# Hybrid diffusion backbone on one core: modulation moved from the HGRN heads to the merge of D, half of its sums on VectorE, a D chunk between two forget gates

## The chip, the core and the metric

The kernel runs as one program on one core of a Trainium2 chip. The metric is device time in microseconds of one execution; less is better. Engines are named as in the profile: PE (TensorE), DVE (VectorE), ACT (ScalarE), POOL (GpSimd) and SP (SyncE, here the queue that issues most DMAs).

## The reference, cut to what matters

Two trunk layers run on 640 tokens (128 of a prompt, 512 of a sample). The prompt and the sample have their own condition vector, so every modulation coefficient exists twice.

```python
for l in range(DEPTH):                                   # DEPTH = 2, D_MODEL = 1024
    mod = silu(cvec) @ w_ada + b_ada                     # (1024) @ (1024, 3072): shift, scale, gate
    h = x * (1 + scale) + shift
    z = h @ w_in + b_in                                  # 92 chunks of 128 columns
    # A: HGRN, 4 heads: q, i, g and two forget gates ff, fb; a gated scan over the tokens, both ways
    out_a = hgrn(a_q, a_ff, a_fb, a_i, a_g)
    out_b = neighbourhood_attention(b_q, b_k, b_v) * silu(b_g)
    out_c = mla(c_qd, c_kvd, c_kpe) * silu(c_g)
    out_d = d_b * short_conv(d_c * d_x) * silu(d_g)      # 4 chunks of 128 columns
    mixed = sum(sigmoid(merge_n) * (out_n @ w_branch[n]) for n in "ABCD") @ w_out
    x = layer_norm(ALPHA * x + gate * mixed)
```

## The kernel before

Activations lie transposed, 128 features by 640 tokens, in tiles that are split in two column halves of 384 and 256 (`HALVES`). Matrix products run at full float32 quality in three passes: every weight chunk is split by `split` (L160 on ACT, L161 on DVE) into a high part `whi` and a low part `wlo`, and `zmm` (L217) issues for each of 8 row blocks high by high, high by low and low by high, 24 matmuls for a column half. `zchunk` makes one chunk of z that way: it calls `tick`, takes one of two PSUM buffers `g`, issues the 24 matmuls and hands the result to an eviction function, for each half. `mm3` (L208) does the same for the branch and output products.

Side work runs in generators, the streams. Each `tick` advances every stream whose waiting count has run down; a `yield n` asks for n ticks. `hg_mix` (the scan of one HGRN head, 27 ticks), `mla_mix`, `na_all` and `mods` are streams; their instructions stand in the order of the program between two halves of a z chunk. [...]

A layer goes so: four heads, each with its z chunks (`hg_z`) and then its scan as a stream; the D chunks (`branch_d`, four z chunks each) stand after the heads by the table `D_AT`: chunk 0 after head 0, 1 and 2 after head 1, 3 after head 2. Before head h, `need(hgs[h - 2])` ticks until that scan is over. Then the merge of D (8 chunks: a merge gate chunk, then a branch product), the MLA projections, the merge of A, the attention projections, and the merges of C and B, and the output phase.

A forget gate (`ff` in `hg_z`) puts much on DVE for each half: a TENSOR_SCALAR (L447), a RECIPROCAL (L449), a multiply (L450), in layer 1 two more (L453, L454). Head 0 of a layer finds q, i and g made ahead, so that its two gates ff(0) and ff(1) follow each other. A silu eviction is L261 and L262 on DVE behind a Tanh on ACT. In the scan, `ks` (L477) is the first DVE work, PE multiplies it at L489, and each of seven levels has a copy on ACT (L499), a predicated copy (L507) and products (L512 to L518) on DVE.

The modulation `mod_group` makes 512 columns of `silu(c) @ w_ada`: 8 loads of 128x512 (`raw`, L379, from SP's queue), each multiplied by the coefficient of the prompt (j = 0) and of the sample (j = 1) on ACT (L382) and added to two accumulators on POOL (L384), one load a tick; then 8 small matmuls against ones (L391) sum over the partitions. During layer 0 the stream `mods` makes 6 groups (the gates of layer 0, shift and scale of layer 1), during layer 1 two. The stream is added ahead of the first head. The results are needed at `need(mods)`, ahead of the output phase. The tiles `t` (2,560 bytes a partition) come from a pool of `NT_SLOT` slots; a load into a slot waits until the slot's last reader is done.

## Time and profile before

| | us |
|---|---|
| median of 3 runs | 2163.67 (2161.42 to 2163.8) |
| the profiled execution, its own time | 2160.13 |
| span of its instructions | 2158.3 |
| PE busy in the span | 2094.6 (97%) |
| DVE busy | 1387.3 (64%) |
| ACT busy | 904.5 (42%) |
| POOL busy | 273.0 (13%) |
| mean granted TensorE clock | 0.991 |

The span is the time from the first to the last instruction; 1.8 us of the execution lie around it. The share of busy time is an average over stages with different limits, so a stage is read by its own rows.

### The profile page before, as it was taken

The page shows a single profiled execution, that of the slowest core. Times are in us where ns is not written, and L with a number is a line of the kernel's source. Part 1 is how long each engine was busy: PE and PEld are TensorE (multiplying, and loading weights), DVE is VectorE, ACT ScalarE, POOL GpSimd, SP SyncE. Part 2 cuts the span into 40 slices and gives each one's busy share as a digit, 9 for nine tenths or more (in the row PEclk, how much of TensorE's full clock was granted, in tenths as well). Part 3 has the DMA queues.
Part 4 walks back from the last instruction along what each step waited for, and adds up shares of the span by engine and source line. Part 5 has one row for each costly group of instructions (what it writes and reads, how often), then busy time and mean ns, then how long its engine had stood idle before and what let it go on. Part 6 is the DMA issues. An engine that isn't in the chain of part 4 may idle for free.

```text
span 2158.3 us, 35747 instructions
## 1 busy us (share of the span) xinstructions
PE 2094.6 (97%) x14538; PEld 2052.8 (95%) x14538; DVE 1387.3 (64%) x2592; ACT 904.5 (42%) x1587; POOL 273.0 (13%) x212
## 2 busy tenths in 40 slices
PE   7999999999999999999998999999999999999997
PEld 4899999999999999999988899999999999999997
DVE  6897878646655567734588877764475546775456
ACT  4445543323334466523364332332343345653332
POOL 0444451000000023200015200000000002221000
PEclk9999999999999999999999999999999999999998
DMA  7332331122112221222433212112121222221251
GB/s 279 111 110 92 113 114 50 62 73 65 58 57 73 73 62 57 67 72 85 142 120 100 74 62 74 57 57 69 62 75 53 68 59 66 69 68 59 74 166 50
DMA packets 70485, 178.06 MB, mean 82 GB/s; under 512 B 7984, under 2 KB 20912, under 8 KB 70320
## 3 DMA queue, kind: packets, MB, share of 16 engines
q1 hardware_dynamic: 67440, 169.32, 24.3%
q10 hardware_dynamic: 2880, 6.45, 0.9%
q8 instruction: 114, 1.87, 0.4%
q14 instruction: 51, 0.42, 0.1%
HBM read 168.20 MB, written 7.54 MB: 81 GB/s over the span
## 4 chain that ended last, share of the span: by engine, by line
PE 80%; DVE 12%; DMA 3%; ACT 2%; issue 2%; POOL 1%; SPq 0%; ACTq 0%; DVEq 0%; POOLq 0%
PE g L217 47%; PE g L208 15%; PE mx L504 2%; DVE wlo L161 2%; PE mx L744 2%; DMA t<-in_wada 2%; PE mx L959 2%; PE mx L208 1%; PE mx L782 1%; DVE s L449 1%; PE mx L926 1%; PE mx L560 1%; PE mx L217 1%; DVE t L161 1%; PE mx L758 1%
## 5 line engine op out<-in xcount | busy, mean ns | idle before, releaser
L217 PE MATMUL g<-h_hi,whi 128*128 128x256 f32 (+1 forms) x2880 | 907.5, 315 | 21.8 <-DVE e L261 10.4
L217 PE MATMUL g<-h_lo,whi 128*128 128x256 f32 (+1 forms) x2880 | 893.9, 310 | 1.1 <-DVE h_lo L409 0.7
L217 PE MATMUL g<-h_hi,wlo 128*128 128x256 f32 (+1 forms) x2880 | 892.7, 310 | 0.6 <-DVE wlo L161 0.6
L217 PEld LDWEIGHTS g<-h_hi,whi 128*128 128x128 f32 x2880 | 549.5, 191 | 27.9 <-DVE e L261 11.9
L217 PEld LDWEIGHTS g<-h_lo,whi 128*128 128x128 f32 x2880 | 550.1, 191 | 3.3 <-DVE h_lo L409 1.5
L217 PEld LDWEIGHTS g<-h_hi,wlo 128*128 128x128 f32 x2880 | 549.4, 191 | 1.0 <-DVE wlo L161 1.0
L161 DVE TENSOR_TENSOR wlo<-wraw,whi 128x1024 fp32r<-128x1024 f32 (+1 forms) x258 | 294.0, 1140 | 312.9 <-ACT whi L160 311.7
L160 ACT CAST whi<-wraw 128x1024 fp32r<-128x1024 f32 (+1 forms) x258 | 242.5, 940 | 443.6 <-PE g L217 250.9
L208 PE MATMUL g<-t,whi 128*128 128x256 f32 (+1 forms) x1280 | 283.4, 311 | 0.0
L882 POOL TENSOR_SCALAR u<-u,sm 128x320 f32<-128x320 f32 (+2 forms) x80 | 90.1, 1137 | 1230.2 <-DVE sm L880 770.7
L208 PEld LDWEIGHTS g<-t,whi 128*128 128x128 f32 x1280 | 214.5, 189 | 0.5
L384 POOL TENSOR_TENSOR t<-t 128x512 f32<-128x512 f32 x112 | 173.4, 1573 | 272.7 <-ACT t L382 272.5
L208 PE MATMUL g<-t,wlo 128*128 128x384 f32 (+1 forms) x640 | 197.7, 309 | 0.0
L208 PEld LDWEIGHTS g<-t,wlo 128*128 128x128 f32 x640 | 121.1, 189 | 0.0
L382 ACT ACTIVATE t<-t,cf 128x512 f32<-128x512 f32 x128 | 90.5, 719 | 71.4 <-DMA t<-in_wada 70.2
L997 ACT ACTIVATE e<-g,hbin 128x384 f32<-128x384 f32 (+1 forms) x128 | 67.1, 524 | 126.8 <-PE g L217 126.7
L504 PE MATMUL mx<-s,t 128*128 128x128 f32 x560 | 78.5, 289 | 1.4 <-DVE s L516 1.3
L504 PEld LDWEIGHTS mx<-s,t 128*128 128x128 f32 x560 | 74.0, 194 | 2.3 <-ACT e L260 1.6
L260 ACT ACTIVATE e<-g,hbin 128x384 f32<-128x384 f32 x76 | 39.9, 525 | 86.1 <-PE g L217 77.1
L449 DVE RECIPROCAL s<-e 128x384 f32<-128x384 f32 (+1 forms) x32 | 68.7, 2147 | 0.6
L261 DVE TENSOR_SCALAR e<-g,vecs 128x384 f32<-128x384 f32 x76 | 41.2, 542 | 39.3 <-ACT e L260 38.9
L807 ACT ACTIVATE t<-mx,sm,rq 128x640 f32<-128x640 f32 (+1 forms) x40 | 31.9, 798 | 70.2 <-DVE sm L804 60.4
(280 smaller groups left out, 2678.1 us busy)
## 6 DMA issues: line engine op xcount, KB each, us to landing
wraw<-in_win SPq DMA_DIRECT2D x184, 512.0 KB, 3.5
t<-in_wada SPq DMA_DIRECT2D x64, 256.0 KB, 3.9
wraw<-in_wbr SPq DMA_DIRECT2D x64, 256.0 KB, 2.6
wraw<-in_wout SPq DMA_DIRECT2D x20, 512.0 KB, 4.3
s<-in_wada SPq DMA_DIRECT2D x16, 512.0 KB, 6.8
s<-in_nabias SPq DMA_DIRECT2D x8, 640.0 KB, 4.7
m<-in_xT SPq DMA_DIRECT2D x8, 320.0 KB, 8.0
t<-in_xT ACTq DMA_DIRECT2D x8, 320.0 KB, 4.9
```

The source lines that it names most:

```text
L160: nc.scalar.copy(hi, raw)
L161: nc.vector.tensor_tensor(lo, raw, hi.bitcast(F32), ALU.subtract)
L208: nc.tensor.matmul(o, wsl(a, k), xsl(b, k, i), start=(k == 0 and p == 0), stop=(k == nk - 1 and p == 2))
L217: nc.tensor.matmul(ps[:, :e - a], at(u, k), v[:, k, a:e], start=(k == 0 and i == 0), stop=(k == 7 and i == 2))
L382: nc.scalar.activation(pr[j], raw, AF.Copy, scale=self.cf[:, k, j:j + 1])
L384: nc.gpsimd.tensor_tensor(acc[j], acc[j], pr[j], ALU.add)
L449: nc.vector.reciprocal(g, r)
L504: nc.tensor.matmul(ps[:, j * 128:(j + 1) * 128], km[:, j * 128:(j + 1) * 128], ap_of(RQ, j * 128, [[2 * B, 64 // B], [T + B, 2], [1, B]]), ...
L744: nc.tensor.matmul(ps[:, e * 512:e * 512 + NH], a, b[:, e * NH:(e + 1) * NH], start=(n == 0), stop=(n == 4))
L882: NORM(nc).tensor_scalar(p[e], p[e], sums[:, e:e + 1], None, ALU.mult)
L959: nc.tensor.matmul(o, x[0:sz], y[0:sz, i, :], start=(i == 0 and n == 0), stop=(i == 2 and n == 2))
L997: self.zchunk(l, "merge", n * 8 + c, lambda ps, p, sl: nc.scalar.activation(th[p], ps, AF.Tanh, bias=hb, scale=0.5))
```

## The change

It does six things. `mods` is added after the fourth head, ahead of the merge of D, and gives up its ticks until the third head's scan (`hgs[2]`) is over. In `mod_group` the prompt's accumulator is kept by DVE: from the second load on, one SCALAR_TENSOR_TENSOR (new L385) multiplies the load and adds it, where ACT multiplied and POOL added. The sample's product is written over the load itself by ACT (L386), and POOL adds it (L387). `branch_d` becomes the generator `branch_d_z`, which stops once after the two chunks d_x and d_c; head 0 runs that first part between ff(0) and ff(1) and the rest (the convolution, d_b, d_g) behind ff(1), so that chunk 0 of D stands ahead of the scan of head 0 and `D_AT[0]` is empty. `NT_SLOT` goes from 25 to 31. A scratch buffer for DMAs of a kind that this program doesn't issue shrinks from its default size to 1,024 bytes.

```diff
@@ -377,11 +377,14 @@
         for k in range(8):
             raw = self.t([128, 512])
             nc.sync.dma_start(raw, self.I["wada"][l, g, k // 2, :, k % 2, :])
-            pr = acc if k == 0 else (self.t([128, 512]), raw)
-            for j in range(2):
-                nc.scalar.activation(pr[j], raw, AF.Copy, scale=self.cf[:, k, j:j + 1])
-                if k:
-                    nc.gpsimd.tensor_tensor(acc[j], acc[j], pr[j], ALU.add)
+            cf = lambda j: self.cf[:, k, j:j + 1]
+            if k == 0:
+                for j in range(2):
+                    nc.scalar.activation(acc[j], raw, AF.Copy, scale=cf(j))
+            else:
+                nc.vector.scalar_tensor_tensor(acc[0], raw, cf(0), acc[0], ALU.mult, ALU.add)
+                nc.scalar.activation(raw, raw, AF.Copy, scale=cf(1))
+                nc.gpsimd.tensor_tensor(acc[1], acc[1], raw, ALU.add)
             yield 1
         yield 1
         ps = self.mx()
@@ -410,12 +413,17 @@
 
 
     def branch_d(self, l, c, out):
+        for _ in self.branch_d_z(l, c, out):
+            pass
+
+    def branch_d_z(self, l, c, out):
         nc = self.nc
         xb = self.bias_chunk(l, "d_x", c)
         u = self.t()
         b = self.bin(l, "d_c", c)
         self.zchunk(l, "d_c", c, lambda ps, p, sl: nc.vector.scalar_tensor_tensor(
             u[:, sl], ps, b, xb[:, sl], ALU.add, ALU.mult))
+        yield
         cw = lambda j: self.vec("conv", (l * 3 + j) * 4 + c)
         y = self.t()
         nc.scalar.activation(y, u, AF.Copy, scale=cw(1))
@@ -434,7 +442,7 @@
         out[c] = y
 
 
-    def hg_z(self, l, h):
+    def hg_z(self, l, h, between=()):
         nc = self.nc
         G = self.s()
         RK = self.s()
@@ -465,7 +473,11 @@
             vT = self.bias_chunk(l, "a_i", h)
             sg = self.silu_chunk(l, "a_g", h)
             ff(0)
+            for _ in between:
+                break
             ff(1)
+            for _ in between:
+                pass
         return G, RK, RQ, q, vT, sg
 
     def hg_mix(self, l, h, z, out):
@@ -1206,7 +1218,9 @@
     def alloc_m(self):
         self.m = self.bp.tile([128, 8, T], F32, name="m")
 
-    def mods(self, todo):
+    def mods(self, todo, after):
+        while self.busy(after):
+            yield 1
         for l, g in todo:
             yield from self.mod_group(l, g)
             yield MOD_GAP
@@ -1219,17 +1233,17 @@
         todo = [(l, 4), (l, 5)]
         if l + 1 < L:
             todo += [(l + 1, g) for g in range(4)]
-        mods = self.add(self.mods(todo))
         for h in range(4):
             if h >= 2:
                 self.need(hgs[h - 2])
-            z = self.hg_z(l, h)
+            z = self.hg_z(l, h, self.branch_d_z(l, 0, oD))
             if l == 0 and h == 0:
                 self.setup_tables()
                 self.ahead = W_AHEAD
             hgs.append(self.add(self.hg_mix(l, h, z, oA)))
             for c in D_AT[h]:
                 self.branch_d(l, c, oD)
+        mods = self.add(self.mods(todo, hgs[2]))
         self.merge(l, 3, oD, first=True)
         z = self.mla_z(l)
         csg = {}
@@ -1259,7 +1273,7 @@
 
 
 FIRST = (("a_q", 0), ("a_i", 0), ("a_g", 0))
-NT_SLOT = 25
+NT_SLOT = 31
 NE_SLOT = 4
 NU_SLOT = 9
 NS_SLOT = 5
@@ -1279,7 +1293,7 @@
 NHL = 2
 HG_WAIT = 2
 HG_W0 = 3
-D_AT = ((0,), (1, 2), (3,), ())
+D_AT = ((), (1, 2), (3,), ())
 MOD_GAP = 1
 
 
@@ -1380,7 +1394,7 @@
     from concourse.bass_utils import run_bass_kernel_spmd as _run
 
     feed = _layout({k: np.asarray(v) for k, v in inputs.items()})
-    nc = _bacc.Bacc("TRN2", target_bir_lowering=False, num_devices=1)
+    nc = _bacc.Bacc("TRN2", target_bir_lowering=False, num_devices=1, dynamic_dma_scratch_size=1024)
     I = {k: nc.dram_tensor(f"in_{k}", v.shape, mybir.dt.from_np(v.dtype), kind="ExternalInput").ap()
          for k, v in feed.items()}
     O = {k: nc.dram_tensor(f"out_{k}", s, F32, kind="ExternalOutput").ap() for k, s in _OUTS.items()}
```

Three places of the order show it. First DVE in head 0 of layer 0, from the second half of ff(0) on. L447, L449 and L450 are the forget gate (L455, L457 and L458 in the changed program), L161 is the low part of a weight chunk, L493 belongs to the scan. Before:

```order
L447 TENSOR_SCALAR e<-e 128x256
L449 RECIPROCAL s<-e 128x256
L450 SCALAR_TENSOR_TENSOR s<-e,s 128x256
L493 TENSOR_TENSOR s<-t,s 128x640
L447 TENSOR_SCALAR e<-e 128x384
L311 CAST masks<-s 128x896
L449 RECIPROCAL s<-e 128x384
L161 TENSOR_TENSOR wlo<-wraw,whi 128x1024
L450 SCALAR_TENSOR_TENSOR s<-e,s 128x384
L447 TENSOR_SCALAR e<-e 128x256
L449 RECIPROCAL s<-e 128x256
L450 SCALAR_TENSOR_TENSOR s<-e,s 128x256
```

Now (L424 evicts d_c, L431 and L432 are the convolution of D):

```order
L455 TENSOR_SCALAR e<-e 128x256
L457 RECIPROCAL s<-e 128x256
L458 SCALAR_TENSOR_TENSOR s<-e,s 128x256
L311 CAST masks<-s 128x896
L161 TENSOR_TENSOR wlo<-wraw,whi 128x1024
L424 SCALAR_TENSOR_TENSOR t<-g,vecs,t 128x384
L424 SCALAR_TENSOR_TENSOR t<-g,vecs,t 128x256
L161 TENSOR_TENSOR wlo<-wraw,whi 128x1024
L431 SCALAR_TENSOR_TENSOR t<-t,vecs 128x127
L431 SCALAR_TENSOR_TENSOR t<-t,vecs 128x511
L432 SCALAR_TENSOR_TENSOR t<-t,vecs 128x127
L432 SCALAR_TENSOR_TENSOR t<-t,vecs 128x511
```

Eight rows came in between the two gates: the weight splits of d_x and d_c, the two evictions of d_c and the four products of the convolution. L493 went behind them.

Second SP's queue behind the first head of layer 0: loads of `w_in` chunks (L167) and of modulation (L379) alternate before:

```order
L379 DMA t<-in_wada 128x512 x2
L167 DMA wraw<-in_win 128x1024
L379 DMA t<-in_wada 128x512
L167 DMA wraw<-in_win 128x1024
L379 DMA t<-in_wada 128x512 x2
L167 DMA wraw<-in_win 128x1024
L379 DMA t<-in_wada 128x512
L167 DMA wraw<-in_win 128x1024
L379 DMA t<-in_wada 128x512
L167 DMA wraw<-in_win 128x1024
```

The rows of the merge of D in the changed program, where the modulation loads stand now:

```order
L167 DMA wraw<-in_win 128x1024
L379 DMA t<-in_wada 128x512 x5
L167 DMA wraw<-in_wbr 128x512
L167 DMA wraw<-in_win 128x1024
L379 DMA t<-in_wada 128x512 x4
L167 DMA wraw<-in_wbr 128x512
L167 DMA wraw<-in_win 128x1024
L167 DMA wraw<-in_wbr 128x512
```

The loads came from among the chunks of the heads to the merge of D, several behind each other, with loads of `w_branch` around them.

Third DVE in the merge of A of layer 0, where `mla_mix` begins. L161 on `t` are low parts of MLA operands, L651 and L654 (now L663 and L666) the normalised latent, L611 (now L623) the rotary embedding. Before:

```order
L161 TENSOR_TENSOR wlo<-wraw,whi 128x512
L261 TENSOR_SCALAR e<-g,vecs 128x256
L161 TENSOR_TENSOR t<-t 128x640
L262 SCALAR_TENSOR_TENSOR t<-e 128x256
L651 TENSOR_TENSOR t<-t,mx 128x512
L654 TENSOR_TENSOR u<-t,mx 128x128
L611 TENSOR_TENSOR e<-t,cs 32x256
L663 COPY u<-t 128x128
L161 TENSOR_TENSOR u<-u 128x128
L611 TENSOR_TENSOR e<-t,cs 32x256 x5
```

Now:

```order
L161 TENSOR_TENSOR t<-t 128x640
L262 SCALAR_TENSOR_TENSOR t<-e 128x256
L161 TENSOR_TENSOR t<-t 128x640
L663 TENSOR_TENSOR t<-t,mx 128x512
L666 TENSOR_TENSOR u<-t,mx 128x128
L623 TENSOR_TENSOR e<-t,cs 32x256
L675 COPY u<-t 128x128
L161 TENSOR_TENSOR u<-u 128x128
L623 TENSOR_TENSOR e<-t,cs 32x256
L385 SCALAR_TENSOR_TENSOR t<-t,cf 128x512
L623 TENSOR_TENSOR e<-t,cs 32x256 x2
L161 TENSOR_TENSOR t<-t 128x640
```

A modulation step (L385) came in; six more of the same group stand within the 62 rows around it.

## Rows read from the trace of the kernel before

**Rows 1.** The page, part 1: busy time of each engine in us, its share of the span, the number of instructions.

```profile
PE 2094.6 (97%) x14538; PEld 2052.8 (95%) x14538; DVE 1387.3 (64%) x2592; ACT 904.5 (42%) x1587; POOL 273.0 (13%) x212
```

**Rows 2.** Busy time by stretch: the stretch and its length in us, then for PE, its weight loads, DVE, ACT and POOL the busy time and in brackets the number of instructions, the granted TensorE clock as a share of full speed, the share of the DMA engines, GB/s. 72 to 350 are the four HGRN heads of layer 0 with the D chunks between them, 350 to 510 the merge of D and the first MLA projections, 510 to 660 most of the merge of A and what follows; 1125 to 1225 the first head of layer 1 and the work behind it, 1225 to 1400 the rest of its heads and most of its merge of D.

```profile
72.00:350.00 278.00, 264.06 (x1846) 261.76 (x1846) 233.26 (x323) 135.48 (x204) 131.95 (x84) 0.98 0.31 102
350.00:510.00 160.00, 160.00 (x1146) 159.93 (x1145) 85.08 (x162) 49.66 (x76) 0.00 (x0) 1.00 0.21 63
510.00:525.00 15.00, 14.60 (x105) 14.34 (x103) 14.53 (x37) 7.47 (x13) 0.00 (x0) 1.00 0.19 58
525.00:540.00 15.00, 14.34 (x100) 14.34 (x101) 9.87 (x23) 5.59 (x9) 0.00 (x0) 1.00 0.25 80
540.00:555.00 15.00, 15.00 (x102) 14.76 (x101) 12.57 (x26) 6.96 (x15) 0.00 (x0) 1.00 0.23 67
555.00:660.00 105.00, 103.68 (x735) 103.18 (x734) 57.30 (x111) 38.02 (x66) 0.00 (x0) 1.00 0.20 62
1125.00:1225.00 100.00, 89.37 (x590) 87.54 (x589) 90.14 (x116) 45.67 (x69) 41.46 (x28) 0.95 0.29 97
1225.00:1400.00 175.00, 175.00 (x1255) 174.90 (x1254) 125.56 (x223) 53.39 (x77) 0.00 (x0) 1.00 0.21 65
```

**Rows 3.** Waits of PE between 72 and 350 us: the waiting tile and line, what it waited for, us in total, times, longest (three of six rows).

```profile
PE g L217 <- DVE e L261: 7.1, 4, 3.0
PE mx L489 <- DVE t L477: 2.9, 1, 2.9
PE mx L391 <- POOL t L384: 1.5, 3, 1.0
```

**Rows 4.** The same between 1125 and 1225 us (three of five rows).

```profile
PE mx L489 <- DVE t L477: 4.4, 1, 4.4
PE g L217 <- DVE e L261: 3.3, 2, 3.0
...
PE mx L391 <- POOL t L384: 0.5, 1, 0.5
```

**Rows 5.** DVE in order of time in the last HGRN head of layer 0: start, us, instruction, output and inputs, shapes.

```profile
303.16 1.23 DVE L161 TENSOR_TENSOR wlo<-wraw,whi 128x1024 fp32r<-128x1024 f32 x1 [0.80 <-ACT whi L160]
...
315.09 1.18 DVE L512 TENSOR_TENSOR s<-s,t 128x320 f32<-128x320 f32 x1
316.18 2.32 DVE L161 TENSOR_TENSOR wlo<-wraw,whi 128x1024 fp32r<-128x1024 f32 x1
318.42 1.55 DVE L514 TENSOR_TENSOR s<-s,t 128x320 f32<-128x320 f32 x1
...
321.05 0.61 DVE L261 TENSOR_SCALAR e<-g,vecs 128x384 f32<-128x384 f32 x1
...
331.34 0.48 DVE L512 TENSOR_TENSOR s<-s,u 128x320 f32<-128x320 f32 x1
```

**Rows 6.** POOL in the same stretch; x4 are four instructions end to end.

```profile
312.30 7.32 POOL L384 TENSOR_TENSOR t<-t 128x512 f32<-128x512 f32 x4 [0.98 <-ACT t L382]
321.55 1.29 POOL L384 TENSOR_TENSOR t<-t 128x512 f32<-128x512 f32 x1 [1.93 <-ACT t L382]
```

**Rows 7.** PE in the same stretch; in brackets how long it stood before this instruction and what for.

```profile
321.72 0.45 PE L217 MATMUL g<-h_hi,whi 128*128 128x384 f32 x1 [3.04 <-DVE e L261]
```

**Rows 8.** Groups of DVE instructions by shape, three of 72 to 350 us and then six of 1225 to 1400 us: line, operation, output and inputs, shapes, count, busy us, mean ns of one, idle time before.

```profile
L161 DVE TENSOR_TENSOR wlo<-wraw,whi 128x1024 fp32r<-128x1024 f32 x29 | 45.1, 1554 | 16.8 <-ACT whi L160 16.8
L449 DVE RECIPROCAL s<-e 128x384 f32<-128x384 f32 x7 | 17.8, 2545 | 0.1
L512 DVE TENSOR_TENSOR s<-s,u 128x320 f32<-128x320 f32 x14 | 10.9, 778 | 2.8 <-ACT t L499 2.8
...
L161 DVE TENSOR_TENSOR wlo<-wraw,whi 128x1024 fp32r<-128x1024 f32 x20 | 24.5, 1223 | 22.1 <-ACT whi L160 22.1
L449 DVE RECIPROCAL s<-e 128x384 f32<-128x384 f32 x4 | 10.2, 2553 | 0.1
L512 DVE TENSOR_TENSOR s<-s,u 128x320 f32<-128x320 f32 x9 | 4.4, 484 | 0.0
L516 DVE TENSOR_TENSOR s<-s,u 128x640 f32<-128x640 f32 x8 | 6.5, 814 | 0.0
L507 DVE COPY_PREDICATED t<-masks,mx 128x640 f32<-128x640 uint8 x12 | 10.5, 875 | 3.5 <-PE mx L504 3.5
L424 DVE SCALAR_TENSOR_TENSOR t<-t,vecs 128x511 f32<-128x511 f32 x3 | 2.2, 744 | 0.0
```

**Rows 9.** PE in order of time, four matmuls of one shape behind a wait that ended at 90.14 us.

```profile
93.05 0.41 PE L217 MATMUL g<-h_hi,whi 128*128 128x256 f32 x1
93.27 0.41 PE L217 MATMUL g<-h_lo,whi 128*128 128x256 f32 x1
...
95.36 0.28 PE L217 MATMUL g<-h_hi,whi 128*128 128x256 f32 x1
95.48 0.28 PE L217 MATMUL g<-h_lo,whi 128*128 128x256 f32 x1
```

**Rows 10.** The page, part 5 (two groups, columns as in rows 8; the last ones are the idle time of the engine before them and what ended it) and part 6 (DMA issues: queue, count, KB each, median us from issue to landing).

```profile
L384 POOL TENSOR_TENSOR t<-t 128x512 f32<-128x512 f32 x112 | 173.4, 1573 | 272.7 <-ACT t L382 272.5
L382 ACT ACTIVATE t<-t,cf 128x512 f32<-128x512 f32 x128 | 90.5, 719 | 71.4 <-DMA t<-in_wada 70.2
...
t<-in_wada SPq DMA_DIRECT2D x64, 256.0 KB, 3.9
```

## Prediction

> **What bounds the kernel now.** The page's first part comes first: PE is busy 97% of the span, DVE 64% [rows 1]. An idle DVE share would make nothing of a change on DVE, but the share is a mean over stages, so the next view is the table by stretch [rows 2]. Subtract PE's busy time from each stretch's length. In 72 to 350 us PE stands 13.94 us, in 1125 to 1225 it stands 10.63 us; in 350 to 510 and in 1225 to 1400 it stands 0.00. The two bad stretches are the ones with POOL at work on the modulation (84 and 28 adds, 131.95 and 41.46 us); the two good ones have none. DVE's share goes with it: 233.26/278 = 84% and 90% there, 53% and 72% in the good ones. The stretch 1225 to 1400 is the control: it holds the same head code and D chunks as layer 0's heads, and PE never waits.
>
> Then the waits: of 13.94 us in the first stretch 7.1 are for a silu eviction on DVE (L261), 2.9 for `ks` (L477), 1.5 for POOL's add itself [rows 3]; in the second 4.4, 3.3 and 0.5 [rows 4]. So DVE is late, mostly. Why, the order of time shows. Four adds run end to end on POOL from 312.30 to 319.62 [rows 6]. In that time the L512 product takes 1.18 us, a weight split 2.32, L514 1.55; beside them the same forms take 0.48 and 1.23 [rows 5]. The excess is 0.70 + 1.09 + 1.07 = 2.86 us, and L261 behind them lets PE go after 3.04 us of waiting [rows 7]. One wait is thus nearly whole the excess of three instructions. Over the stretch the split takes 1554 ns where the control has 1223, L512 778 where it has 484, while the reciprocal takes 2545 against 2553 [rows 8]: some forms are held, others not.
>
> A last piece is the clock. After the wait that ended at 90.14 us matmuls of 256 columns start 0.22 us apart, at 95.36 again 0.12 [rows 9]. [...]
>
> **What can be had at most.** In 350 to 510 PE makes 1146 matmuls in 160 us, 139.6 ns each; the control makes one in 139.4. At that pace the 1846 and 590 matmuls of the bad stretches need 257.7 and 82.4 us, so they lose 20.3 + 17.6 = 38 us: 24.6 standing, 9 at the lower clock, 4 in getting under way again. The widths are not mixed alike everywhere, so this is an estimate.
>
> **The change part by part.**
> The adds leave the heads, all 112 of them. If that makes the heads like the control, 38 us come back. I leave 6 of them. Half is for the two D chunks behind head 1: chunk 0 has gone ahead of the scan of head 0, so these 16 ticks now hold 17 ticks of that scan instead of 9, with a second scan beside it. Eight ticks are four levels, each of 0.87 (L507) + 2 x 0.48 (L512 and L514, one shape) + 0.81 (L516) = 2.64 us of DVE at the control's durations [rows 8], so 11 us more in some 65; the 32 adds that ran in 16 ticks held DVE by 32 x 0.47 = 15 us (0.47 below). In layer 0 it comes out even, in layer 1 DVE has 11 us more than in the control, 72% + 17%. The other half is a third of the loss at the lower clock. Bounds: 0 and, if the doubled scans wait as the heads do now (20.3/278 of 130 us), 10, plus the 3 for the clock.
>
> The D chunk between the gates of head 0 adds no instruction. It takes from DVE the two gates in a row (each half has a reciprocal of 2.55 us [rows 8]) ahead of `ks`, on which the two long waits for L477 lie; they are in the 38 already. The first scan has 26 ticks till `need` where it takes 27, so one tick stands without a chunk; two column halves still lie between its last two steps, as before. Nothing.
>
> On DVE 56 new SCALAR_TENSOR_TENSORs of 128x512 come in. The nearest row is L424, same operation, 511 columns: 744 ns [rows 8], 41.7 us in all. ACT loses 56 of 128 products, 40 us at 719 ns, POOL 56 adds [rows 10]. ACT is at 42% [rows 1] and waits more than it is waited for: nothing.
>
> The 56 adds that remain now hold DVE in the merges. What an add costs DVE: its share is 84% and 90% against 72% in the control, (0.121 x 278 + 0.183 x 100)/112 = 52.1/112 = 0.47 us; a held instruction pays up to 1.07 (L514 above). A step costs DVE 0.744 + 0.47 = 1.2 us. The 42 steps of layer 0 stand between the fifth chunk of the merge of D and the attention projections, so 51 us go into 350 to 660, where DVE has 310 - 179.35 = 131 us free [rows 2]: 74% on the mean, the control's level, hidden. In one place cover is missing: at the start of `mla_mix` DVE is busy 14.53 of 15 us and PE already stands 0.40 and 0.66 us [rows 2]. The order puts seven steps of the third group round it, three within. 3 x 1.2 = 3.6 us, say 4 with what is behind (the branch eviction L1024, a weight split). From below 0, as the scheduler has some play; from above 7 x (0.744 + 1.07) = 12.7.
>
> [...]
>
> Each group still ends with PE waiting for the last add, as now (1.5 + 0.5 us for eight groups [rows 3, 4]); the third group's matmuls stand closest behind their last step. 2 us, between 0 and 6.
>
> Six more slots and the smaller scratch cost no instruction; SP's loads of weights have a lead of three buffers.
>
> **The sum.** 38 - 6 - 4 - 2 = 26 us. The profiled execution took 2160.1, so 2134 by its measure; it lies 3.5 below the median of the three runs, 2163.67, for which I forecast 2138.
>
> **The rivals.**
> *The waits only move.* DVE's overload at `mla_mix` and the held instructions in the merges reach PE at the upper bounds: 12.7 + 6, and 10 + 3 stay in the heads: 38 - 31.7, a gain of 6, 2157. For it: DVE at 97% for 15 us there. Against it: before, DVE's full 15 us cost PE only 0.40.
>
> *DVE stands for the loads; slower.* ACT stood 70.2 us for modulation loads in 128 instructions [rows 10], and the longest waits of PE name DVE and POOL all the same [rows 3, 4]. Now the first reader of 56 of 64 loads is DVE, and behind it in its queue are weight splits and PSUM evictions on which PE hangs. If the loads were as late as now, DVE would stand 70.2 x 56/64 = 61 us. It has 131 - 51 = 80 us free, so PE need not see it; from 26 us passed on to PE the gain is gone and beyond that the change is slower; with all of it 2138 + 61 = 2199. Against it: a load lands 3.9 us after issue [rows 10], the DMA engines are at 0.21 there against 0.31 [rows 2], six more slots let loads go earlier, and SP's order puts four or five loads together ahead of their steps.
>
> *It doesn't do what it says.* The heads would wait for DVE anyway, by reciprocals and scans: then only POOL's own 2 us go, 2162 to 2166. Against it stands the control stretch.
>
> **How the numbers follow.** Forecast (gain 12 to 38, so 2126 to 2152, 2138 the likeliest): 0.75. Waits move (2152 to 2159): 0.11. No change: 0.06. Loads stall DVE: 0.08. The range for 8 in 10 goes from the full 38 us without a new wait, 2125, to the waits-move case, 2156. A difference of 0.2% (4.3 us) is about what a measurement of this kernel can tell from none. Faster by more: 0.86; within: 0.06; slower: 0.08.
>
> **What would show it.** Right: no adds in the heads; the split near 1.22 and L512 near 0.48 there; PE standing under 5 us in layer 0's heads, no wait for L477; clock near 1.00; DVE 70 to 75% in the heads of layer 0; new PE waits, 3 to 8 us, by the start of `mla_mix` and at the ones matmuls. Wrong: waits for DVE evictions in the D chunks behind head 1; DVE idle for in_wada by tens of us in the merges; the overtime of DVE's products staying without adds beside them.

## The result, and the profile after

The changed kernel takes 2148.54 us (median of 4 runs, 2147.71 to 2149.83), the kernel before 2163.74 beside it: a ratio of 0.9935, with a 95% interval of 0.9922 to 0.9948. That is 14 us faster by the ratio, 0.65%; forecast were 26 us, 2138 in a range from 2125 to 2156. Direction and range held, the size did not, and the runs below show that the reason given for the gain was only half right. The profiled execution of after took 2149.83 us, its span is 2148.0.

The table by stretch again, of the changed kernel (us; busy time and count of PE, its weight loads, DVE, ACT, POOL; granted clock; DMA share and GB/s), which answers to [rows 2]:

```profile
72.00:350.00 278.00, 278.00 (x1976) 277.86 (x1976) 203.45 (x326) 88.34 (x130) 0.00 (x0) 1.00 0.22 66
350.00:510.00 160.00, 154.41 (x1086) 153.68 (x1085) 105.03 (x201) 62.20 (x97) 30.39 (x20) 0.98 0.32 100
510.00:525.00 15.00, 12.73 (x76) 12.03 (x74) 7.54 (x19) 4.08 (x6) 1.28 (x1) 0.90 0.26 86
...
540.00:555.00 15.00, 13.11 (x95) 12.87 (x94) 12.79 (x23) 7.04 (x14) 4.49 (x4) 1.00 0.30 95
555.00:660.00 105.00, 102.44 (x720) 101.74 (x720) 66.04 (x123) 45.35 (x79) 17.56 (x14) 0.98 0.29 95
1125.00:1225.00 100.00, 100.00 (x700) 99.97 (x700) 76.19 (x118) 31.90 (x46) 0.00 (x0) 1.00 0.25 75
```

In the heads of both layers PE now stands for nothing: it is busy 278.00 of 278.00 us and 100.00 of 100.00, at a granted clock of 1.00, with DVE at 73 and 76%. It makes 240 more matmuls there than before (1976 and 700 for 1846 and 590), some 34 us at 0.14 each. That is nearly all that was lost. But from 350 to 660 us, where PE had hardly stood [rows 2], it stands 12.3 us (5.59 + 2.27 + 1.89 + 2.56), and the granted clock is below 1.00 in three of the four stretches shown. The waits of PE in 350 to 660 us, by line and by what ended them (us in total, times, longest):

```profile
PE g L217 <- DVE e L1024: 3.9, 2, 2.1
PE g L208 <- ACT e L1009: 3.6, 2, 2.3
PE mx L756 <- ACT t L819: 2.4, 2, 1.9
PE mx L516 <- DVE s L528: 2.0, 1, 2.0
PE mx L394 <- POOL t L387: 0.5, 1, 0.5
```

L1009 is the tanh of the merge gate and L1024 the multiplication by it, both out of PSUM; L528 is the last product over all tokens in a scan step, L819 the exponential in the latent attention's softmax; L394 are the ones matmuls. Half of these waits end with ACT, an engine that the change relieved. The modulation's own groups (line, engine, shapes, count, busy us, mean ns, idle time before and what ended it) show why; in the changed kernel L385 is the new step on DVE, L386 the product on ACT, L387 the add on POOL:

```profile
L385 DVE SCALAR_TENSOR_TENSOR t<-t,cf 128x512 f32<-128x512 f32 x56 | 51.8, 925 | 20.5 <-DMA t<-in_wada 20.2
L386 ACT ACTIVATE t<-t,cf 128x512 f32<-128x512 f32 x56 | 40.0, 720 | 44.8 <-DVE t L385 28.8 <-DVE sm L193 5.6 <-POOL t L387 4.5
L387 POOL TENSOR_TENSOR t<-t 128x512 f32<-128x512 f32 x56 | 79.7, 1423 | 1017.0 <-ACT t L386 1016.0
```

ACT waits 28.8 us for DVE's step. L386 writes its product over `raw`, and L385 must have read `raw` first: in the code of before both readers were on ACT, and there was no such wait. What it does, first on ACT, then on DVE, POOL and PE, at one place (start, us, engine, instruction, idle time before):

```profile
393.88 0.72 ACT L386 ACTIVATE t<-t,cf 128x512 f32<-128x512 f32 x1 [1.22 <-DVE t L385]
394.51 1.03 ACT L160 CAST whi<-wraw 128x1024 fp32r<-128x1024 f32 x1
395.44 0.47 ACT L1009 ACTIVATE e<-g,hbin 128x256 f32<-128x256 f32 x1
```

```profile
394.16 2.42 DVE L385 SCALAR_TENSOR_TENSOR t<-t,cf 128x512 f32<-128x512 f32 x2
396.50 1.21 DVE L161 TENSOR_TENSOR wlo<-wraw,whi 128x1024 fp32r<-128x1024 f32 x1
397.64 0.87 DVE L519 COPY_PREDICATED t<-masks,mx 128x640 f32<-128x640 uint8 x1
398.40 1.13 DVE L528 TENSOR_TENSOR s<-s,u 128x640 f32<-128x640 f32 x1
```

```profile
394.74 1.29 POOL L387 TENSOR_TENSOR t<-t 128x512 f32<-128x512 f32 x1 [3.60 <-ACT t L386]
396.66 4.00 POOL L387 TENSOR_TENSOR t<-t 128x512 f32<-128x512 f32 x2 [0.63 <-ACT t L386]
```

```profile
395.96 0.51 PE L208 MATMUL g<-t,whi 128*128 128x256 f32 x2 [1.30 <-ACT e L1009]
399.68 0.68 PE L516 MATMUL mx<-s,t 128*128 128x128 f32 x4 [2.02 <-DVE s L528]
```

L386 stands 1.22 us for DVE; the weight cast and the tanh that follow it on ACT without a gap are late by that (the last matmul of the tanh's input had started at 391.16 us, the tanh starts at 395.44), and PE waits 1.30 us for the tanh. Beside it the old mechanism: two steps take 2.42 us with an add on POOL beside them (a pair takes 1.41 where there are no adds, in all_dve below); the next add holds L528, 1.13 us for 0.81; PE waits 2.02 us for L528.

### The profile page after: what moved, and what is told of

It reads as the page before. It is cut to its first block, busy times and chain, and to the rows that moved or that the text cites. A ratio compares the mean times of both kernels' runs of the same rounds, so it can differ in the third digit from the quotient of the medians.

```text
span 2148.0 us, 35645 instructions
## 1 busy us (share of the span) xinstructions
PE 2095.0 (98%) x14538; PEld 2055.4 (96%) x14538; DVE 1378.0 (64%) x2648; ACT 867.1 (40%) x1531; POOL 179.1 (8%) x156
## 4 chain that ended last, share of the span: by engine, by line
PE 87%; DVE 7%; issue 2%; ACT 2%; DMA 2%; POOL 0%; SPq 0%; DVEq 0%; ACTq 0%; POOLq 0%
PE g L217 55%; PE g L208 13%; PE mx L516 3%; PE mx L756 2%; PE mx L971 2%; PE mx L208 1%; PE mx L794 1%; PE mx L217 1%; DVE wlo L161 1%; PE mx L938 1%; PE mx L572 1%; DVE t L161 1%; PE mx L770 1%; PE mx L549 1%; PE mx L394 1%
## 5 line engine op out<-in xcount | busy, mean ns | idle before, releaser
L217 PE MATMUL g<-h_hi,whi 128*128 128x256 f32 (+1 forms) x2880 | 905.2, 315 | 10.7 <-DVE e L1024 6.9
L217 PE MATMUL g<-h_lo,whi 128*128 128x256 f32 (+1 forms) x2880 | 893.5, 310 | 2.2 <-DVE h_lo L412 2.1
L217 PE MATMUL g<-h_hi,wlo 128*128 128x256 f32 (+1 forms) x2880 | 892.9, 310 | 0.6 <-DVE wlo L161 0.6
L217 PEld LDWEIGHTS g<-h_hi,whi 128*128 128x128 f32 x2880 | 548.1, 190 | 14.7 <-DVE e L1024 8.0
L217 PEld LDWEIGHTS g<-h_lo,whi 128*128 128x128 f32 x2880 | 549.0, 191 | 3.7 <-DVE h_lo L412 2.7
L217 PEld LDWEIGHTS g<-h_hi,wlo 128*128 128x128 f32 x2880 | 548.5, 190 | 1.0 <-DVE wlo L161 1.0
L161 DVE TENSOR_TENSOR wlo<-wraw,whi 128x1024 fp32r<-128x1024 f32 (+1 forms) x258 | 285.1, 1105 | 279.6 <-ACT whi L160 277.9
L208 PE MATMUL g<-t,whi 128*128 128x256 f32 (+1 forms) x1280 | 284.7, 312 | 4.9 <-ACT e L1009 4.9
L208 PEld LDWEIGHTS g<-t,whi 128*128 128x128 f32 x1280 | 215.3, 190 | 6.2 <-ACT e L1009 5.7
L208 PE MATMUL g<-t,wlo 128*128 128x384 f32 (+1 forms) x640 | 198.3, 310 | 0.0
L387 POOL TENSOR_TENSOR t<-t 128x512 f32<-128x512 f32 x56 | 79.7, 1423 | 1017.0 <-ACT t L386 1016.0
L208 PEld LDWEIGHTS g<-t,wlo 128*128 128x128 f32 x640 | 121.5, 190 | 0.0
L1009 ACT ACTIVATE e<-g,hbin 128x384 f32<-128x384 f32 (+1 forms) x128 | 66.9, 523 | 116.0 <-PE g L217 115.9
L457 DVE RECIPROCAL s<-e 128x384 f32<-128x384 f32 (+1 forms) x32 | 68.9, 2152 | 0.9
L385 DVE SCALAR_TENSOR_TENSOR t<-t,cf 128x512 f32<-128x512 f32 x56 | 51.8, 925 | 20.5 <-DMA t<-in_wada 20.2
L519 DVE COPY_PREDICATED t<-masks,mx 128x640 f32<-128x640 uint8 x56 | 49.0, 876 | 23.8 <-PE mx L516 23.8
```

What stands on the lines that cost most here:

```text
L161: nc.vector.tensor_tensor(lo, raw, hi.bitcast(F32), ALU.subtract)
L208: nc.tensor.matmul(o, wsl(a, k), xsl(b, k, i), start=(k == 0 and p == 0), stop=(k == nk - 1 and p == 2))
L217: nc.tensor.matmul(ps[:, :e - a], at(u, k), v[:, k, a:e], start=(k == 0 and i == 0), stop=(k == 7 and i == 2))
L385: nc.vector.scalar_tensor_tensor(acc[0], raw, cf(0), acc[0], ALU.mult, ALU.add)
L387: nc.gpsimd.tensor_tensor(acc[1], acc[1], raw, ALU.add)
L457: nc.vector.reciprocal(g, r)
```

## The experiments

Two theories stood at first: that the new waits come from ACT's product standing behind DVE's step (A), or from the adds that still hold DVE (B); a third was the loads (C). All kernels are the changed one with the edit shown (late_own, late_old, late_dve, pause_dve, heads_dve and no_sums start from another experiment, which is named), and each was timed in 4 to 12 runs beside the kernel before on the same chip. The changed kernel itself was not run again, so it is compared through the ratio to before, each of which has an interval of about 0.0015 to either side.

**own_tile**: ACT writes the product elsewhere and goes first.

```
+                pr = self.t([128, 512])
+                nc.scalar.activation(pr, raw, AF.Copy, scale=cf(1))
                 nc.vector.scalar_tensor_tensor(acc[0], raw, cf(0), acc[0], ALU.mult, ALU.add)
-                nc.scalar.activation(raw, raw, AF.Copy, scale=cf(1))
-                nc.gpsimd.tensor_tensor(acc[1], acc[1], raw, ALU.add)
+                nc.gpsimd.tensor_tensor(acc[1], acc[1], pr, ALU.add)
```

> The changed kernel, but ACT writes the sample's product into a tile of its own and is issued ahead of DVE's SCALAR_TENSOR_TENSOR, so that it no longer overwrites the raw tile that DVE still has to read. Theory A (the new waits in the merges come from ACT's in-place product standing behind DVE's step, 28.8 us in 19 waits, with a weight cast and a tanh eviction behind it in ACT's queue): ACT's idle time ahead of L386 that ends with DVE goes, the PE waits for tanh evictions (L208 for e of L1009, 4.9 us, and L756 for L819, 2.4 us) go, and the time falls from 2148.5 to about 2141. Rival B (DVE is held by POOL's adds and is late by itself): within 2 us of 2148.5, the PE waits unchanged. Rival C (DVE stands for late loads, 20.2 us): no change either, DVE's 20.2 us of standing stay.

2140.21 us, ratio 0.9896 (0.9879 to 0.9914): 8 us better than the change. ACT no longer waits for the step, PE's waits for the tanh are gone, and those for DVE stay. PE's waits in 350 to 660 us, two of four rows (the step is L387 here, the multiplication by the tanh L1025):

```profile
PE g L217 <- DVE e L1025: 5.5, 2, 3.4
PE mx L395 <- DVE t L387: 2.3, 1, 2.3
```

Theory A holds for its part of the loss. The tile and the order were changed together, so what each is worth alone is not shown.

**place_only** (the move with the old arithmetic: two products on ACT, two adds on POOL) and **stt_in_heads** (the new arithmetic at the old place).

```
place_only, in mod_group:
-            if k == 0:
-                for j in range(2):
-                    nc.scalar.activation(acc[j], raw, AF.Copy, scale=cf(j))
-            else:
-                nc.vector.scalar_tensor_tensor(acc[0], raw, cf(0), acc[0], ALU.mult, ALU.add)
-                nc.scalar.activation(raw, raw, AF.Copy, scale=cf(1))
-                nc.gpsimd.tensor_tensor(acc[1], acc[1], raw, ALU.add)
+            pr = acc if k == 0 else (self.t([128, 512]), raw)
+            for j in range(2):
+                nc.scalar.activation(pr[j], raw, AF.Copy, scale=self.cf[:, k, j:j + 1])
+                if k:
+                    nc.gpsimd.tensor_tensor(acc[j], acc[j], pr[j], ALU.add)

stt_in_heads, in layer:
+        mods = self.add(self.mods(todo, None))
         for h in range(4):
...
-        mods = self.add(self.mods(todo, hgs[2]))
```

> The changed kernel with the old arithmetic of the modulation: both products on ACT, both sums on POOL (112 adds in the merges, no step on DVE). Theory A: DVE no longer stands for loads and ACT no longer for DVE, so most of the some 18 us of new loss in the merges goes: about 2136. Rival B: 112 adds hold DVE by 112 x 0.47 = 53 us where 56 steps with their adds cost it 56 x 1.2 = 68 us, so the loss in the merges falls only by that ratio, to some 14 us: about 2144, and more waits for POOL's last add ahead of the ones matmuls.

> The changed kernel with the modulation back in the heads (the stream starts ahead of the first head, as before), with the new arithmetic. Theory (what counts in the heads is how much of DVE the modulation takes, step and hold together): 56 x 1.2 = 68 us where 112 adds took 53, so the heads lose 38 x 68/53 = 49 us instead of 5, the merges get their 18 back: 2148.5 + 44 - 18, about 2175, slower than the kernel before. Rival (only the held instructions count, and half the adds hold half as many): the heads lose 19, 2148.5 + 14 - 18, about 2145.

place_only: 2156.25 us, ratio 0.9976 (0.9966 to 0.9986). stt_in_heads: 2147.99, ratio 0.9936 (0.9921 to 0.9950), the same as the change. The first is slower than either theory said, the second follows the rival. The move alone is worth 5 us; the new arithmetic alone is worth all 14, and moving it on top of that nothing. That comparison has the tie between ACT and DVE in it: in stt_in_heads ACT stands 58.1 us for the step, twice what it does in the change. A tile of its own in the heads was not tried, so what the move would be worth with one is open. Theory A can't be the whole cause: place_only has no step on DVE, and loses more in the merges. What it has more of is adds, 112 for 56. The rows of place_only for 350 to 510 and 510 to 660 us:

```profile
350.00:510.00 160.00, 155.09 (x1086) 153.51 (x1084) 97.41 (x172) 74.05 (x114) 58.01 (x40) 0.98 0.31 97
510.00:660.00 150.00, 140.04 (x938) 137.50 (x939) 92.80 (x172) 72.65 (x127) 46.32 (x34) 0.95 0.28 90
```

DVE is at 61% there, and PE stands 14.9 us. At one of these places, from 391 to 398 us, adds run on POOL and four DVE products (L521, L523, L161, L525) take 1.13, 1.58, 1.68 and 1.88 us, where their forms take 0.48, 0.48, 1.22 and 0.81 in the control [rows 8]: 3.3 us more in all. PE stands 2.69 us there, for L1019, which comes next on DVE.

**d_undone**: chunk 0 of branch D back behind head 0.

```
-            z = self.hg_z(l, h, self.branch_d_z(l, 0, oD))
+            z = self.hg_z(l, h)
-D_AT = ((), (1, 2), (3,), ())
+D_AT = ((0,), (1, 2), (3,), ())
```

> The changed kernel with the first D chunk back behind head 0 instead of between its two forget gates. By the forecast the move is worth nothing: within 2 us of 2148.5. Rival 1 (it is what took the waits for ks away from layer 0's first heads, 2.9 us): 2151 to 2152. Rival 2 (it takes 11 us of DVE work from behind head 1): 2143 to 2146.

2148.87 us, ratio 0.9937 (0.9924 to 0.9949): worth nothing that can be measured, as forecast.

**all_dve**: both sums on DVE, no adds and, behind the first, no product on ACT.

```
-                nc.vector.scalar_tensor_tensor(acc[0], raw, cf(0), acc[0], ALU.mult, ALU.add)
-                nc.scalar.activation(raw, raw, AF.Copy, scale=cf(1))
-                nc.gpsimd.tensor_tensor(acc[1], acc[1], raw, ALU.add)
+                for j in range(2):
+                    nc.vector.scalar_tensor_tensor(acc[j], raw, cf(j), acc[j], ALU.mult, ALU.add)
```

> The changed kernel at its own place, but both sums are made by SCALAR_TENSOR_TENSOR on DVE: no adds on POOL, no product on ACT behind the first. Theory (DVE's burden at the place counts): 112 steps of 0.75 us are 84 us where 56 steps with their adds took 68; the loss of 23 grows to 28, less the some 7 that the coupling with ACT cost: about 2147. Rival 1 (what reaches PE is single instructions held for one or two us by an add): without adds the DVE products fall back to their free durations and most of the loss goes, about 2135. Rival 2 (loads: two steps of DVE now stand behind each load): slower, 2155 or more.

2135.35 us, ratio 0.9876 (0.9862 to 0.9889): 13 us better than the change, with 56 more steps on DVE. Rival 1: a step falls back to 745 ns (925 with the adds), and the waits at 396 and 399 us are gone. Of the 7.9 us that PE still stands in 350 to 660 us, 6.0 lie at one place (of L217's 5.2 the longest, and L208's):

```profile
PE g L217 <- DVE e L1022: 5.2, 2, 3.8
PE g L208 <- ACT e L1007: 2.2, 1, 2.2
```

The 3.8 us end at 507 us, the 2.2 at 499. DVE before them, in order of time (the steps are L385 again; L621, of 32 partitions, is part of the rotation of the latent attention's keys and queries):

```profile
497.00 1.41 DVE L385 SCALAR_TENSOR_TENSOR t<-t,cf 128x512 f32<-128x512 f32 x2
498.35 1.23 DVE L161 TENSOR_TENSOR wlo<-wraw,whi 128x1024 fp32r<-128x1024 f32 x1
...
502.75 1.71 DVE L621 TENSOR_TENSOR e<-t,cs 32x256 f32<-32x256 f32 x4
...
506.44 0.55 DVE L1022 SCALAR_TENSOR_TENSOR e<-e,g 128x384 f32<-128x384 f32 x1
```

DVE stands 0.79 us in these 9.4; the steps, a weight split and the rotation are all ahead of the L1022 that PE waits for.

**pause_dve**: all_dve, and no step for 14 ticks at that place.

```
         for k in range(8):
+            while self.hold:
+                self.hold -= 1
+                yield 1
...
+        self.hold = 14
         z = self.mla_z(l)
```

> all_dve, but the modulation steps pause for 14 ticks from the projections of the latent attention on, so that none stands where DVE rotates its keys and queries (L617 to L623, DVE full at 490 to 510 us). Theory (the 2.2 and 3.8 us of waiting at 499 and 507 us and their like in layer 1 come from the steps and loads in DVE's queue there): about 6 us less, 2129. Rival (the place is full without them): within 2 us of 2135.

2129.18 us, ratio 0.9851 (0.9837 to 0.9864): 6 us less than all_dve, as expected (5 by the ratios, with about 4 to either side), and the fastest of the kernels that make the sums, 1.5% faster than the kernel before and 0.8% faster than the change. From 350 to 660 us PE stands 2.05 us:

```profile
350.00:510.00 160.00, 159.08 (x1138) 158.64 (x1137) 103.08 (x215) 52.47 (x81) 0.00 (x0) 1.00 0.29 90
510.00:660.00 150.00, 148.87 (x1048) 147.14 (x1047) 109.91 (x218) 58.80 (x109) 0.00 (x0) 1.00 0.31 103
```

**heads_dve**: the arithmetic of all_dve at the old place, by the edit of stt_in_heads.

> The arithmetic of all_dve (both sums on DVE, no adds) at the old place: the stream starts ahead of the first head. Theory (with the adds gone DVE's room decides the place: heads of layer 0 have DVE at 203 of 273 us without modulation, and 84 steps of 0.75 us are 63 us, 97% together): slower than all_dve by 15 to 25, about 2155. Rival (the place is worth nothing with this arithmetic either, as it was with the mixed one, 2148.0 against 2148.5): 2135.

2136.29 us, ratio 0.9878 (0.9863 to 0.9894), the same as all_dve. My theory of DVE's room fell again, and this run is the clearest of all. First stt_in_heads, then heads_dve, from 72 to 350 us: the stretch, and of DVE the groups of the weight split, the step, the reciprocal and the last product of a scan step.

```profile
72.00:350.00 278.00, 268.93 (x1886) 267.13 (x1885) 238.16 (x370) 112.84 (x167) 67.57 (x42) 0.98 0.31 102
...
L161 DVE TENSOR_TENSOR wlo<-wraw,whi 128x1024 fp32r<-128x1024 f32 x31 | 39.9, 1286 | 8.2 <-ACT whi L160 8.2
L385 DVE SCALAR_TENSOR_TENSOR t<-t,cf 128x512 f32<-128x512 f32 x42 | 38.4, 914 | 7.1 <-DMA t<-in_wada 7.0
L457 DVE RECIPROCAL s<-e 128x384 f32<-128x384 f32 x7 | 17.8, 2547 | 0.2
L528 DVE TENSOR_TENSOR s<-s,u 128x640 f32<-128x640 f32 x13 | 12.2, 941 | 0.0
```

```profile
72.00:350.00 278.00, 276.60 (x1977) 275.52 (x1976) 247.28 (x423) 89.63 (x130) 0.00 (x0) 1.00 0.33 108
...
L385 DVE SCALAR_TENSOR_TENSOR t<-t,cf 128x512 f32<-128x512 f32 x84 | 59.3, 740 | 0.7 <-DMA t<-in_wada 0.5
L161 DVE TENSOR_TENSOR wlo<-wraw,whi 128x1024 fp32r<-128x1024 f32 x32 | 38.9, 1218 | 13.6 <-ACT whi L160 13.6
L455 DVE RECIPROCAL s<-e 128x384 f32<-128x384 f32 x8 | 20.4, 2548 | 0.1
L526 DVE TENSOR_TENSOR s<-s,u 128x640 f32<-128x640 f32 x14 | 11.4, 814 | 0.0
```

DVE is fuller, 247 us for 238 (89% for 86%), and PE stands 1.40 us instead of 9.07. The kernel before had DVE at 84% and stood 13.94 [rows 2]. In the heads it was not DVE's share that made PE wait. Elsewhere a full DVE did: the waits that pause_dve takes away (7.9 us in 350 to 660 us become 2.05) have no add beside them.

**late_own**, **late_old**, **late_dve**: own_tile, place_only and all_dve with the steps started before the third projection of the neighbourhood branch, beside the end of the latent attention and the merges of C and B.

```
-        mods = self.add(self.mods(todo, hgs[2]))
...
             if c == 2:
+                mods = self.add(self.mods(todo, None))
                 self.need(mla)
```

> The kernel own_tile, with the modulation stream started not in the merge of D but before the third projection of the neighbourhood branch, so that its 42 steps of layer 0 run beside the end of the latent attention and the merges of C and B. Theory (the loss sits where DVE has no room: in own_tile 3.4 us of waiting for L1025 and 2.3 us for the last sum come at 506 and 519 us, where DVE is full even without modulation, 14.53 of 15 us; from 915 to 1020 it has 42 of 105 us of work): the some 12 us lost in 475 to 550 go, some 3 come back beside the attention: 2140 falls to about 2130. Rival (a step costs PE the same wherever it stands, as heads and merges did): 2140, within 2.

> The kernel place_only (old arithmetic: two products on ACT, two sums on POOL), started at the same late place. Theory: what the 112 adds cost is DVE's room at the place; of the some 36 us that place_only loses in the merges of both layers about 10 stay: 2156 falls to about 2132, close to late_own. Rival (the adds hold DVE wherever they stand, and the hold reaches PE): above 2148.

> The arithmetic of all_dve at the late place of late_own. Theory (late_own gained nothing over after because its adds stand in POOL's queue ahead of the attention's copies, 8.7 us of waits for L895, and hold the DVE evictions L1025, 8.4 us): without adds these waits go, 2149 falls to about 2132, as good as all_dve or better. Rival (the late place is itself too full): 2140 or more.

late_own: 2149.42, ratio 0.9939 (0.9927 to 0.9952). late_old: 2159.02, 0.9984 (0.9974 to 0.9994). late_dve: 2148.07, 0.9934 (0.9922 to 0.9947). By the ratios they are 9, 2 and 12 us behind their sisters at the merge of D (the 2 within the noise); the theory failed in all three. The place has a chain of its own that the table of DVE's busy time does not show. In late_dve, PE's longest sum of waits, then DVE, POOL and PE at one of them:

```profile
PE mx L936 <- POOL u L892: 11.6, 13, 2.5
```

```profile
840.98 0.75 DVE L385 SCALAR_TENSOR_TENSOR t<-t,cf 128x512 f32<-128x512 f32 x1
...
842.64 0.15 DVE L890 RECIPROCAL sm<-sm 128x2 f32<-128x2 f32 x1
...
842.97 0.74 DVE L385 SCALAR_TENSOR_TENSOR t<-t,cf 128x512 f32<-128x512 f32 x1
...
844.29 1.40 DVE L385 SCALAR_TENSOR_TENSOR t<-t,cf 128x512 f32<-128x512 f32 x2
```

```profile
842.96 4.90 POOL L892 TENSOR_SCALAR u<-u,sm 128x384 f32<-128x384 f32 x2 [5.08 <-DVE sm L890]
```

```profile
847.91 0.55 PE L936 MATMUL mx<-ident,u 128*128 128x128 f32 x3 [2.54 <-POOL u L892]
```

Here PE depends on POOL's scaling of the probabilities, which starts when DVE's reciprocal of the sums (0.15 us) has been made. A step of 0.75 us stands ahead of the reciprocal. The larger part comes behind it: beside the steps from 842.97 us on, the two scalings take 4.90 us. In the kernel before, the same two take about half:

```profile
767.93 2.47 POOL L882 TENSOR_SCALAR u<-u,sm 128x384 f32<-128x384 f32 x2 [2.78 <-DVE sm L880]
```

The 2.43 us more are nearly all of the 2.54 that PE stands: as products on DVE took longer beside adds, so these scalings on POOL took longer beside steps. Over the whole kernel POOL's 80 scalings take 96.9 us in late_dve and 90.0 before. Only this one of the 13 waits was read in order of time.

**prefetch**: each load issued a tick ahead of its step (the change otherwise, with one tick more in each group).

```
+        nxt = load(0)
+        yield 1
         for k in range(8):
-            raw = self.t([128, 512])
-            nc.sync.dma_start(raw, self.I["wada"][l, g, k // 2, :, k % 2, :])
+            raw = nxt
+            if k < 7:
+                nxt = load(k + 1)
```

> The changed kernel with each modulation load issued one tick (some 5 us) ahead of the step that reads it, a tick more in each group. Theory C (DVE's 20.2 us of standing for loads is what makes it and ACT late): the standing goes, and with it most of ACT's 28.8 us behind DVE: about 2141. Rival (the coupling is through DVE's queue, not the load): DVE's standing for loads goes, but ACT still waits and the time stays within 2 us of 2148.5.

2147.20 us, ratio 0.9934 (0.9920 to 0.9947): nothing. DVE's standing for loads halved, from 20.2 to 10.7 us, ACT's waiting for DVE's step doubled, from 28.8 to 58.9. The loads are not the cause. Nor is the sum of ACT's waits a price: here it doubled at no cost.

**no_sums**: all_dve with the steps left out, the loads kept.

> all_dve without the 112 steps: of each modulation row only the first of its eight parts is used, the other loads are still made and read by nothing. What is left is the time without the sums, the bound for any way of placing them. Theory: the loss by the sums is what was counted in the traces (some 38 us in the kernel before, 23 in the changed one, 12 in all_dve), so 2123 to 2126. Rival (loads and other work take part of it): 2130 or more.

2129.54 us, ratio 0.9850 (0.9836 to 0.9863). The theory (2123 to 2126) was missed; the time lies at the rival's edge. The kernel leaves out the sums, not the loads nor the first two products of each group, so its time is a yardstick and not a bound. By it the sums cost the kernel before 32 us, the changed one 18, all_dve 6, and pause_dve nothing that can be measured.

## Why the forecast was too high

By the ratios to before, the gains in us (of 2163, each with about 3 to either side):

| arithmetic of a step | at the old place, in the heads | at the merge of D | late |
|---|---|---|---|
| two products on ACT, two adds on POOL | 0 (the kernel before) | 5 (place_only) | 3 (late_old) |
| one sum on DVE, one add on POOL | 14 (stt_in_heads) | 14 (the change), 22 with a tile of its own (own_tile) | 13 (late_own, own tile) |
| both sums on DVE | 26 (heads_dve) | 27 (all_dve), 32 with the pause | 14 (late_dve) |

Read down, 112 adds become 56 and none, and each time 9 to 14 us are gained in the first two columns. In the late column the second time gains nothing; one cause that the rows show is that the steps which replace the adds lengthen POOL's scalings there (two at one wait took 4.90 us for 2.47). Read across the first two, the move is worth 5 us with the old arithmetic and nothing with either of the new ones as written; own_tile has no counterpart in the heads. Each step down also takes 56 products off ACT. No run parts that from the adds; for the adds speak the waits, which mostly name DVE [rows 3, 4], and DVE's longer products beside them.

*The heads: 38 less 6.* Right in size: by the count of matmuls the heads have some 34 us back. 32 us is also what no_sums gives as the whole cost of the sums, and after the change the heads have none of it. The D chunks behind head 1 do not wait, for which I had kept half of the 6. But I had taken this for the gain of the move, and it is not: the sums brought more than half of their cost along. The 9 us "at the lower clock" in the 38, the 4 beside them and the 3 kept for the clock, a third of the 9, are terms that no run shows. In the trace of before, 65 matmuls of z chunks with 256 columns start 0.22 us apart between 72 and 350 and between 1125 and 1225 us, where others of the form start 0.12 apart [rows 9]: 6.5 us, an estimate from these spacings; in the changed kernel the granted clock is 1.00 in both stretches.

*The D chunk between the gates, nothing.* Right (d_undone).

*DVE's new steps "in 350 to 660", hidden.* This is the step that failed. I had priced a step at 1.2 us of DVE, 0.744 and 0.47 for the add beside it, set the 51 us against 131 free ones, and called 74% "the control's level, hidden". The price was right: taking the steps out of DVE's times in stt_in_heads and heads_dve leaves 238.16 - 38.4 = 199.8 and 247.28 - 59.3 = 188.0 us (for 328 and 339 other instructions), so 42 adds and their holds on the steps cost DVE 11.8 + 42 x (0.914 - 0.740) = 19.1 us, 0.46 each (an estimate, as the 328 and 339 instructions are not quite the same ones). The argument was wrong. It treated a hold as load that free time absorbs. PE waits for single DVE instructions (L1024, L528 in the merges), and holds in a row ahead of one come out at PE nearly whole where they were read, at 84% load (2.86 us and a wait of 3.04 before, [rows 5 to 7]) as well as at 61% (3.3 and 2.69 in place_only), while PE stands only 1.40 us in the heads beside 84 steps of 0.74 us at 89% load (heads_dve). I had the first pair in the text and went on to reckon with shares. Why a hold reaches PE where a step does not was not tried; that the scheduler sets a step's place in the queue, and a hold falls where it will, is only an argument.

*ACT's fewer products, nothing.* Wrong, and the second part of the miss. The change left ACT less to do, but made `raw` a tile that two engines read and one of them overwrites, and so tied ACT's queue, with casts and tanh evictions in it, to DVE's: 8 us by own_tile, with about 5 to either side. Of the 13 us that all_dve gains on the change this is the larger part. The 4 that are left between own_tile and all_dve are within the noise, so the 56 holds that remained, less what the 56 added steps cost, are not measured by themselves; that holds reach PE is shown by the kernels with 112 adds and no such tie (before, place_only). A step has to be read for the waits it creates on every tile, not for its durations alone.

*The start of `mla_mix`, 4 us (0 to 12.7).* Right: in the changed kernel PE stands 2.27 us there for L1009 (till 505 us) and 1.81 for L1024 (till 512). In all_dve, with two steps to a load, the pause there is worth 6, in both layers together. *The ones matmuls, 2 us.* 0.5 us of waiting in 350 to 660.

So the sum of new cost was 6 (4 + 2) where 18 was measured: all_dve, with neither adds nor the tie, still costs 6, and 13 went to the holds and the tie to ACT, for which the forecast had nothing. That the 6 agree is partly luck, since the arithmetic of all_dve isn't the one forecast. In numbers: 32 - 18 = 14.

*The rivals.* "The waits only move" gave 2157; the change comes half way to it. place_only, the move without the new arithmetic, measured 2156.25 (2154.07 to 2160.79; 2158 by the ratio), but that agreement is luck: the rival left 13 us of waits and clock in the heads, and in place_only PE is busy 278.00 of 278.00 and 98.84 of 100.00 us there. Nearly all its loss is in the merges. "DVE stands for the loads": it does stand, 20.2 us, but prefetch halves that standing and gains nothing by it. "It doesn't do what it says" is out.

Beside adds some forms of DVE took longer, and others did not. The pair of steps at 394.16 us took 2.42 us beside an add of 1.29, 1.0 more than a pair without adds (1.41). From stt_in_heads to heads_dve, that is without the adds, the mean of L161 goes from 1286 to 1218 ns and that of the last product of a scan step from 941 to 814, both with two tensors as inputs; that of the reciprocal, with one, stays (2547 and 2548 ns). What makes the difference no run shows.

## What to carry to other kernels

When instructions of one engine hold another's, count the holds that can fall on an instruction a bound engine waits for, not the share of time they take. Half as many adds gained 9 to 14 us at each of the three places here, no adds 12 and 13 us more at two of the three; moving the 112 gained 5 us. It went the other way too: at one wait of the late place two scalings on POOL took 4.90 us beside steps on DVE, for 2.47 without. When a sum is shared out over engines, look for tiles that one engine reads and another overwrites: a separate tile, written first, was worth 8 us. A table of busy time finds a full place, but not a chain through three engines such as the late place had; try the place, or read who waits for whom there.

## What the runs showed of the hardware

At one place the clock fell without a wait of PE. In heads_dve the trace shows PE busy without a gap from 470 to 510 us (ends of matmuls are modelled), yet the granted clock from 490 to 500 is 0.66. The stretch, and of PE in order of time the matmuls ahead of it:

```profile
490.00:500.00 10.00, 10.00 (x49) 10.00 (x50) 4.64 (x23) 0.63 (x3) 0.00 (x0) 0.66 0.10 28
...
489.03 2.29 PE L643 MATMUL mx<-ones,t 128*128 128x2 f32 x20
491.19 2.14 PE L646 MATMUL mx<-ones,t 128*128 128x2 f32 x10
```

Thirty matmuls of 2 columns (L643, L646) run from 489.03 to 493.19 us, and behind them matmuls of 384 columns start 0.32 us apart until 498.13, then 0.17. So here 4.2 us of matmuls of 2 columns went ahead of the slower pace, as a wait of 2.9 us [rows 3] did that ended at 90.14 us in the kernel before [rows 9]. The kernel before runs the same matmuls (L633, L636) near 505 us with the clock at 1.00 [rows 2], the ten of the second group in less time:

```profile
504.97 1.26 PE L636 MATMUL mx<-ones,t 128*128 128x2 f32 x10
```

What decides it stays open. It cost some 2 us, an estimate from the spacing (15 matmuls, 0.32 for 0.17 us each). It is one place in one trace.
